# A two-layer encoder trunk: one transfer for four weight blocks, a fixed order of the MLP's products, narrower projection products, and products ahead of the head whose result nobody reads

## The chip, the cores and the metric

The kernel runs on one core of a Trainium2 chip. The metric is the device time of one execution in microseconds (us). The profile is one execution, taken by the hardware profiler. In it PE is TensorE's products, PEld its loading of stationary operands, DVE VectorE, ACT ScalarE, POOL GpSimd and SP SyncE, which issues most transfers.

## The reference

```python
def reference(x, mem, mem_norm, attn_norm, mlp_norm, a_w_in, a_rpb, b_w_in, b_q_norm,
              b_k_norm, w_mem_kv, w_o, w_up, w_down, final_norm):
    m = rms_norm(mem, mem_norm)
    h = x
    for i in range(DEPTH):                       # DEPTH = 2
        n = rms_norm(h, attn_norm[i])
        j = i // N_MIXERS
        if i % N_MIXERS == 0:
            z = n @ a_w_in[j]                    # 2048 x 5120
            q, k, v, qm = jnp.split(z, [MIX_WIDTH, 2 * MIX_WIDTH, 3 * MIX_WIDTH], axis=-1)
            mix = neighbourhood_attention(...)   # 12 heads of 128, learned relative bias
        else:
            z = n @ b_w_in[j]                    # 2048 x 3072
            ...
            mix = gqa_block_attention(q, k, split_heads(v, N_KV_HEADS))
        km, vm = jnp.split(m @ w_mem_kv[i], 2, axis=-1)
        cross = memory_attention(...)            # 4 heads into 256 memory tokens
        h = h + jnp.concatenate([mix, cross], axis=-1) @ w_o[i]
        n = rms_norm(h, mlp_norm[i])
        h = h + jnp.square(jax.nn.relu(n @ w_up[i])) @ w_down[i]   # 2048 x 8192 and back
    return rms_norm(h, final_norm)
```

All is float32, with 256 tokens of width 2048.

## The kernel before

Every matrix product is made of three products of a rounded type: each operand is split into a high part (a rounding copy on ScalarE) and a low part (the difference, on VectorE), and high by high, high by low and low by high are added up in PSUM. The function `split` issues this pair; in the profile all of its copies stand on line 329 and all of its differences on line 330. Weights come in chunks of 128 x 2048 (1 MB), are loaded by SP's queue, split in two halves, and used once.

The work is a list of grains. A grain runs a part of a chunk's products; ahead of it, by a fixed number of grains, its load is issued (8 ahead), its sums (`pre`, 5 ahead) and its split (4 ahead). A scheduler may then move instructions on each engine; `pin` keeps an instruction in the program's order on its engine.

There are three kinds of products. An **S** chunk gives 128 output features for all 256 tokens: the weights are stationary, the activations move, and for each of 16 k-tiles (`s_products`, lines 240 to 251) there is one 512-wide product of the weights' high part with both parts of the activations (line 247) and one 256-wide product of the low part (line 250). The two halves of the PSUM tile are then added by `summed` (lines 368 to 376). There are 36 such chunks: the memory keys of both layers, and queries, keys and memory queries of layer A. An **M** chunk has the activations stationary and the weights moving, 512 wide (lines 234, 237, 238): values, all of layer B's projections, the output projection and the last part of the MLP's way down. In the **MLP** (`up_grains`, `down_grains`) the way up is like an S chunk, but with three 256-wide products a k-tile (lines 735 and 736). The way down uses a scheme with seven products in place of eight (names p1 to p7, lines 849 to 851), on sums of weight blocks.

The hidden width is cut in eight parts. The first part's up chunks stand alone; then come 56 steps a layer, each with one up chunk (48 products, 256 wide) and one down step (21 products, 512 wide). A down step takes four weight blocks of 128 x 512. Three of them are loaded into `b` (768 KB), the fourth into `t` (256 KB). `pre` adds one block to the fourth on VectorE (line 828) and lets a transfer of POOL's queue add another one in place (line 829, called the accumulating transfer here). `prep_first` splits the three blocks (bh, bl), `prep_second` makes two more sums (lines 837, 838) and splits four (th, tl). Both tiles have two buffers in turn; bh, bl, th and tl have one each. The first products (three names, nine products) use bh and bl, the second (four names, twelve products) th and tl.

At the start, `begin` splits the memory tokens and the first three S chunks in quarters. Their loads are issued by SP in the order written; the first quarter of each of the three weight chunks is issued by ScalarE (line 142).

Of the kernel before, what the change touches and what calls it, by code (L numbers as in the profile page):

```python
# [17 lines left out]
P = 128  # L18
# [17 lines left out]
GROUP = 2  # L36
# [8 lines left out]
LAST_AT = 224  # L45
MASKED = -1e30
# [21 lines left out]
class Shifted:  # L68
# [5 lines left out]
    def __getitem__(self, key):  # L74
        _, k, s = key
        at = k * 512 + (s.start or 0)
        if k == KT - 1:

            at = k * 512 + (0 if s.start else SEQ + LAST_AT // 4)
        return self.room[:, at : at + SEQ]  # L80

# [9 lines left out]
def encoder_kernel(ctx: ExitStack, tc: tile.TileContext, t: dict, out: bass.AP):  # L91
# [62 lines left out]
    nc.scalar.activation(warm, mhalf[:, :1], AF.Exp)  # L154

# [10 lines left out]
    def halves_of(w):  # L166
# [9 lines left out]
        def prep(hf):  # L176
# [7 lines left out]
            tiles[hf] = new_half()  # L184
            split(*tiles[hf], tiles["raw"][:, hf * HALF : (hf + 1) * HALF])
# [23 lines left out]
    def new_half():  # L209
        return (at.ring.tile([P, HALF], F32R, tag="hi", bufs=4, name="hi"),  # L210
                at.ring.tile([P, HALF], F32R, tag="lo", bufs=4, name="lo"))
# [28 lines left out]
    def s_products(w, k0, nk, hi, lo):  # L240

        acts, ps = w.acts(), w.ps
        for j0 in range(0, nk, GROUP):
            js = range(j0, min(j0 + GROUP, nk))
            for j in js:
                s = slice(j * P, (j + 1) * P)
                nc.tensor.matmul(ps, hi[:, s], acts[:, k0 + j, :], start=k0 + j == 0, stop=False)  # L247
            for j in js:
                s = slice(j * P, (j + 1) * P)
                nc.tensor.matmul(ps[:, SEQ:], lo[:, s], acts[:, k0 + j, :SEQ], start=False,  # L250
                                     stop=k0 + j == KT - 1)

    def begin():
# [5 lines left out]
        for q in range(4):  # L259
            for k in range(4 * q, 4 * q + 4):  # L260
                split_pair(box["memT"], mem0[:, k * SEQ : (k + 1) * SEQ], G_MEM, k)
                if k % 4 == 0:
                    for c, w in enumerate(plan[:FIRST_CHUNKS]):
                        if q % 2 == 0:
                            tiles[c] = new_half()
# [33 lines left out]
    def add_s(src, acts, done):  # L299
        def start(w):  # L300
            w.ps = at.acc.tile([P, 512], F32, tag="acc", name="ps_s")
# [66 lines left out]
    def summed(ps, name, row=None, factor=1.0):  # L368

        a = at.work.tile([P, SEQ], F32, tag="sum_a", name=f"{name}_a")  # L370
        nc.scalar.activation(a, ps[:, SEQ:], AF.Copy)
        s = at.work.tile([P, SEQ], F32, tag="sum_s", name=f"{name}_s")
        nc.vector.tensor_tensor(s, ps[:, :SEQ], a, op=ALU.add)
        if row is not None:
            nc.vector.scalar_tensor_tensor(s, s, factor, row, op0=ALU.mult, op1=ALU.mult)
# [142 lines left out]
    def add_mem(layer):  # L518
        for hd in range(NMH):
            add_s(t[f"w_km{layer}"][hd], get("memT"), km_done(layer, hd))  # L520
# [206 lines left out]
    def u_products(ps, k0, nk, hi, lo):  # L727

        acts = box["hT"]
        for j in range(nk):  # L730
            k = k0 + j
            s = slice(j * P, (j + 1) * P)
            parts = (slice(0, SEQ), slice(SEQ, 512))
            for n, x in enumerate(parts if k < KT - 1 else parts[::-1]):
                nc.tensor.matmul(ps, hi[:, s], acts[:, k, x], start=k == n == 0, stop=False)  # L735
            nc.tensor.matmul(ps, lo[:, s], acts[:, k, :SEQ], start=False, stop=k == KT - 1)  # L736
# [12 lines left out]
    def up_grains(layer, part, m):  # L749
# [8 lines left out]
        def run(hf):  # L758
            if hf == 0:
                if part == 0:  # L760
                    own["ps"] = at.acc.tile([P, 512], F32, tag="acc", name="ps_u")[:, :SEQ]
                else:
                    if part == 1 and m == 0:
                        closed("ps_att", "ps_acc")
                        at.sums = opened("ps_sums", space=bass.MemoryType.PSUM)
                        box["ps"] = {}
                        box["unused"] = set()
# [513 lines left out]
```

## Time and profile before

| | us |
|---|---|
| median of 3 runs | 2047.32 |
| the runs | 2046.80, 2047.32, 2050.19 |
| the profiled execution's own time | 2048.19 |
| its span, first to last instruction | 2046.4 |

The mean granted TensorE clock of the profiled execution was 0.998. A line of a group gives source line, engine, operation, the tile written and those read, shape and count, then the busy time in us, the mean of one in ns, and the engine's idle time just before them with what ended it. A line of the timeline gives start and length in us, engine, line and what is done, and how many are merged in it. A line of a stretch gives its ends, its length, then busy time and count for each engine, the granted clock, the mean busy share of the DMA engines, and GB/s.

### The profile page before, as it was taken

Reading aid. Unit: us, or ns where it says so; the run is one execution under the profiler, and the core shown is the slowest. Engines: PE = TensorE matmul, PEld = TensorE weight load, DVE = VectorE, ACT = ScalarE, POOL = GpSimd, SP = SyncE. Lnnn points to the kernel's source line nnn. Section 1 sums busy time; section 2 is a strip of 40 time slices with the busy share of each in tenths; the row PEclk is TensorE's granted clock in tenths of the full one; section 3 lists DMA queues with packets and bytes.
Section 4 is the critical chain, followed back from the end, with each engine's and each line's share of the span. In section 5 each row is a group of like instructions: output and inputs, shape, how many; then the busy total and the mean of one; then the engine's idle time right before and its main releaser. Section 6 shows DMA issues by size and latency. Waiting matters only on the chain.

```text
span 2046.4 us, 31582 instructions
## 1 busy us (share of the span) xinstructions
PE 2026.7 (99%) x12516; PEld 1813.8 (89%) x12516; DVE 1667.0 (81%) x2061; ACT 1251.6 (61%) x1652; POOL 119.2 (6%) x144
## 2 busy tenths in 40 slices
PE   8999999999999999999999999999999999999998
PEld 7888888889999999999988888889999999999996
DVE  6767667558989989999897667657998989999996
ACT  6755555556666666666656557556666666666664
POOL 0000000000000000000000001000000000000000
PEclk9999999999999999999999999999999999999999
DMA  7755554727777777787775554536877777777773
GB/s 281 283 190 179 191 177 169 277 80 233 231 231 232 220 232 230 226 242 222 230 222 199 180 185 144 184 125 216 246 227 227 227 231 229 234 232 227 236 221 130
DMA packets 93429, 433.79 MB, mean 212 GB/s; under 512 B 10464, under 2 KB 12128, under 8 KB 60128
## 3 DMA queue, kind: packets, MB, share of 16 engines
q1 hardware_dynamic: 75456, 398.47, 57.3%
q0 software_dynamic: 16816, 31.46, 8.7%
q8 instruction: 98, 1.61, 0.3%
q10 hardware_dynamic: 1008, 1.84, 0.3%
q14 instruction: 51, 0.42, 0.1%
HBM read 398.17 MB, written 4.19 MB: 197 GB/s over the span
## 4 chain that ended last, share of the span: by engine, by line
PE 93%; DVE 3%; DMA 2%; issue 1%; ACT 0%; POOLq 0%; POOL 0%; SPq 0%; DVEq 0%; ACTq 0%
PE ps_u L735 21%; PE ps_u L736 11%; PE ps_m L234 8%; PE ps_m L237 8%; PE ps_m L238 8%; PE p L849 8%; PE p L850 8%; PE p L851 8%; PE ps_s L247 7%; PE ps_s L250 3%; DMA t<-in_w_pair 1%; DVE tl L330 1%; PE pt_a L410 1%; DVE ul L330 1%; PE pt_n L347 1%
## 5 line engine op out<-in xcount | busy, mean ns | idle before, releaser
L735 PE MATMUL ps_u<-hT,uh 128*128 128x256 f32 x4096 | 713.2, 278 | 0.2
L735 PEld LDWEIGHTS ps_u<-hT,uh 128*128 128x128 f32 x4096 | 627.4, 188 | 10.3 <-ACT uh L329 0.6
L736 PE MATMUL ps_u<-hT,ul 128*128 128x256 f32 x2048 | 568.9, 278 | 1.6 <-DVE ul L330 1.5
L329 ACT ACTIVATE uh<-raw_U 128x1024 fp32r<-128x1024 f32 x278 | 294.6, 1061 | 307.1 <-PE ps_u L735 290.0
L330 DVE TENSOR_TENSOR lo<-raw,hi 128x1024 fp32r<-128x1024 f32 (+1 forms) x220 | 261.4, 1194 | 164.5 <-ACT hi L329 162.9
L736 PEld LDWEIGHTS ps_u<-hT,ul 128*128 128x128 f32 x2048 | 386.2, 189 | 4.2 <-DVE ul L330 3.2
L330 DVE TENSOR_TENSOR ul<-raw_U,uh 128x1024 fp32r<-128x1024 f32 x278 | 337.3, 1218 | 40.6 <-ACT uh L329 40.5
L329 ACT ACTIVATE hi<-raw 128x1024 fp32r<-128x1024 f32 (+1 forms) x220 | 227.5, 1039 | 210.2 <-PE ps_m L238 119.1
L329 ACT ACTIVATE th<-t 128x2048 fp32r<-128x2048 f32 x112 | 215.2, 1921 | 118.7 <-PE p L851 107.8
L330 DVE TENSOR_TENSOR tl<-t,th 128x2048 fp32r<-128x2048 f32 x112 | 256.0, 2286 | 23.9 <-ACT th L329 23.5
L330 DVE TENSOR_TENSOR bl<-b,bh 128x1536 fp32r<-128x1536 f32 x112 | 196.0, 1750 | 0.3 <-ACT bh L329 0.3
L850 PE MATMUL p<-tl,a_s 128*128 128x512 f32 x448 | 174.8, 390 | 0.0
L851 PE MATMUL p<-th,a_s 128*128 128x512 f32 x448 | 174.3, 389 | 0.0
L329 ACT ACTIVATE bh<-b 128x1536 fp32r<-128x1536 f32 x112 | 166.2, 1484 | 7.3 <-PE p L851 1.2
L829 POOL DMA_DIRECT2D t<-b x112 | 97.0, 866 | 1158.8 <-DVE t L828 556.0
L849 PE MATMUL p<-th,a_s 128*128 128x512 f32 x448 | 164.1, 391 | 0.0
L247 PE MATMUL ps_s<-nT,hi 128*128 128x512 f32 x448 | 142.5, 397 | 0.0
L851 PE MATMUL p<-bh,a_s 128*128 128x512 f32 x336 | 131.1, 390 | 0.0
L850 PE MATMUL p<-bl,a_s 128*128 128x512 f32 x336 | 131.0, 390 | 0.0
L828 DVE TENSOR_TENSOR t<-t,b 128x512 f32<-128x512 f32 x112 | 77.2, 689 | 57.6 <-DMA t<-in_w_pair 46.5
L849 PE MATMUL p<-bh,a_s 128*128 128x512 f32 x336 | 108.0, 389 | 0.0
L237 PE MATMUL ps_m<-lo,nT 128*128 128x512 f32 x264 | 103.7, 393 | 0.0
(237 smaller groups left out, 3305.1 us busy)
## 6 DMA issues: line engine op xcount, KB each, us to landing
raw_U<-in_w_up SPq DMA_DIRECT2D x128, 1024.0 KB, 6.6
b<-in_w_pair SPq DMA_DIRECT2D x112, 768.0 KB, 4.5
raw<-in_w_o SPq DMA_DIRECT2D x32, 1024.0 KB, 5.0
t<-in_w_pair SPq DMA_DIRECT2D x112, 256.0 KB, 3.4
t<-b POOLq DMA_DIRECT2D x112, 256.0 KB, 6.9
raw<-in_w_b SPq DMA_DIRECT2D x21, 1024.0 KB, 4.9
raw<-in_w_av SPq DMA_DIRECT2D x12, 1024.0 KB, 4.9
raw<-in_w_aq SPq DMA_DIRECT2D x12, 1024.0 KB, 4.9
```

What stands on the lines that cost most here:

```text
L234: first = nc.tensor.matmul(w.ps[i], ah, hi[:, s], start=st, stop=False)
L237: nc.tensor.matmul(w.ps[i], ah, lo[:, s], start=False, stop=False)
L238: nc.tensor.matmul(w.ps[i], al, hi[:, s], start=False, stop=sp)
L247: nc.tensor.matmul(ps, hi[:, s], acts[:, k0 + j, :], start=k0 + j == 0, stop=False)
L329: first = nc.scalar.activation(dst_hi, src, AF.Copy)
L330: return first, nc.vector.tensor_tensor(dst_lo, src, dst_hi.bitcast(F32), op=ALU.subtract)
L735: nc.tensor.matmul(ps, hi[:, s], acts[:, k, x], start=k == n == 0, stop=False)
L736: nc.tensor.matmul(ps, lo[:, s], acts[:, k, :SEQ], start=False, stop=k == KT - 1)
L829: nc.gpsimd.dma_start(s[:, 0, :], block(1), accum_op=ALU.add)
L849: nc.tensor.matmul(ps, a[:, 0, ai, :], hi[:, s], start=begins, stop=False)
L850: nc.tensor.matmul(ps, a[:, 0, ai, :], lo[:, s], start=False, stop=False)
L851: nc.tensor.matmul(ps, a[:, 1, ai, :], hi[:, s], start=False, stop=ends)
```

## The change

- The four blocks of a down step come in one transfer of 1 MB into `b`. All sums are made in `pre`, into a tile `t` of three; the accumulating transfer adds into the fourth block of `b`. The first split takes all four blocks (2048 wide) and the first products are four names (p3, p1, p2, p5); the second split takes three sums (1536 wide) for three names.
- A step's grains are ordered down first, up first half, up second half, down second, and the first product of each group is pinned in the program's order.
- S chunks use the same three 256-wide products as the way up, into one 256-wide sum, so `summed` needs no addition. Their split tiles lie 64 bytes into a somewhat longer buffer. The first half of an S chunk that follows an M chunk starts with its low part, which is laid out apart (`Entered`). Two of the first four chunks share a PSUM bank.
- At the start, SP issues all first loads; twelve 128 x 128 products of a tile of ones are issued ahead of all others, into a PSUM tile that is not read.
- The last part's second chunks are loaded into the buffers of `b` in place of those of `T`.

```diff
             for c in range(FIRST_CHUNKS):
-                (nc.sync if j else nc.scalar).dma_start(raws[c][:, s], t["w_km0"][c][:, s])
+                nc.sync.dma_start(raws[c][:, s], t["w_km0"][c][:, s])
...
+    idle = at.att.tile([P, P], F32, tag="att", name="idle")
+    for _ in range(12):
+        nc.tensor.matmul(idle, ones, ones, start=True, stop=True)
...
+            if w.kind == "S" and hf == 0 and plan[plan.index(w) - 1].kind == "M":
+                tiles[hf] = entered_half(src)
+            else:
+                tiles[hf] = new_half(w.kind)
+                split(*tiles[hf], src)
...
+    def new_half(kind):
+        s = slice(STILL_AT // 4, STILL_AT // 4 + HALF) if kind == "S" else slice(0, HALF)
+        return tuple(at.ring.tile([P, HALF + 64], F32R, tag=n, bufs=4, name=n)[:, s] for n in ("hi", "lo"))
+
+    def entered_half(src):
+        hi = at.ring.tile([P, HALF + 64], F32R, tag="hi", bufs=4, name="hi")[:, STILL_AT // 4 :][:, :HALF]
+        lo = Entered(at.ring.tile([P, HALF + 64], F32R, tag="lo", bufs=4, name="lo"))
+        nc.scalar.activation(hi, src, AF.Copy)
+        for dst, s in ((lo.first, slice(0, P)), (lo.rest, slice(P, HALF))):
+            nc.vector.tensor_tensor(dst, src[:, s], hi[:, s].bitcast(F32), op=ALU.subtract)
+        return hi, lo
...
+    def products(ps, acts, k0, nk, hi, lo, keep_order=False):
+        for j in range(nk):
+            k = k0 + j
+            s = slice(j * P, (j + 1) * P)
+            parts = [(hi, slice(0, SEQ)), (hi, slice(SEQ, 512)), (lo, slice(0, SEQ))]
+            if k == KT - 1:
+                parts[:2] = parts[1::-1]
+            elif j == 0 and isinstance(lo, Entered):
+                parts = parts[2:] + parts[:2]
+            for n, (x, part) in enumerate(parts):
+                ins = nc.tensor.matmul(ps, x[:, s], acts[:, k, part], start=k == n == 0,
+                                       stop=k == KT - 1 and n == 2)
+                if keep_order and n == 0:
+                    pin(ins)
...
-    FIRST = ("p3", 6, 0), ("p1", 0, 1), ("p2", 2, 2)
-    SECOND = ("p5", 3, 0), ("p7", 4, 1), ("p6", 5, 2), ("p4", 1, 3)
+    FIRST = ("p3", 6, 0), ("p1", 0, 1), ("p2", 2, 2), ("p5", 3, 3)
+    SECOND = ("p7", 4, 0), ("p6", 5, 1), ("p4", 1, 2)
...
-            own["b"] = at.side.tile([P, 3 * 512], F32, tag="b", bufs=2, name="b")
-            nc.sync.dma_start(own["b"], src[:, : 3 * 512])
-            own["t"] = at.side.tile([P, 4, 512], F32, tag="T", bufs=2, name="t")
-            nc.sync.dma_start(own["t"][:, 0, :], src[:, 3 * 512 :])
+            own["b"] = at.side.tile([P, 4, 512], F32, tag="b", bufs=2, name="b")
+            nc.sync.dma_start(own["b"].rearrange("p a b -> p (a b)"),
+                              t[f"w_pair{layer}"][(part * 2 + q) * STEPS + j])
...
         def pre():
-            s = own["t"]
-            nc.vector.tensor_tensor(s[:, 1, :], s[:, 0, :], block(0), op=ALU.add)
-            nc.gpsimd.dma_start(s[:, 0, :], block(1), accum_op=ALU.add)
+            b, s = own["b"], at.side.tile([P, 3, 512], F32, tag="T", bufs=2, name="t")
+            nc.vector.tensor_tensor(s[:, 0, :], b[:, 3, :], b[:, 0, :], op=ALU.add)
+            nc.gpsimd.dma_start(b[:, 3, :], b[:, 1, :], accum_op=ALU.add)
+            nc.vector.tensor_tensor(s[:, 1, :], s[:, 0, :], b[:, 1, :], op=ALU.add)
+            nc.vector.tensor_tensor(s[:, 2, :], s[:, 1, :], b[:, 2, :], op=ALU.add)
+            own["t"] = s
...
-            plan.extend((up[0], down[0], up[1], down[1]))
+            plan.extend((down[0], up[0], up[1], down[1]))
```

The switch of the PSUM pools moves from the first up grain of the second part to the first down grain. In the programs as they are built, TensorE's order of an ordinary step is the same circle before and after: before, twelve second products of one step, nine first products of the next, 48 up products; after, twelve first products, 48 up products, nine second products.

More of the change, by code (lines that the diff above doesn't have):

```diff
@@ L762, in run @@
                 else:
[L763 to L767, printed above, removed]
                     own["ps"] = at.sums.tile([P, 512], F32, tag="up", name="ps_u")[:, :SEQ]
[L769 removed]
+            products(own["ps"], box["hT"], hf * (KT // 2), KT // 2, *own.pop(hf), keep_order=part > 0)
         def after():
```

78 lines of the change are left out of this document (30 added, 48 removed).

## The prediction

> **What bounds the kernel now.** I read the page first, then the times of the stretches, then the groups of the MLP stretch, and last the timeline of the places that the change touches. The page says who is busy and what the chain to the end is made of.
>
> ```profile
> span 2046.4 us, 31582 instructions
> PE 2026.7 (99%) x12516; PEld 1813.8 (89%) x12516; DVE 1667.0 (81%) x2061; ACT 1251.6 (61%) x1652; POOL 119.2 (6%) x144
> PE 93%; DVE 3%; DMA 2%; issue 1%; ACT 0%; POOLq 0%; POOL 0%; SPq 0%; DVEq 0%; ACTq 0%
> ```
>
> TensorE sets the time nearly everywhere. A change can gain only by starting TensorE earlier, by spacing its products closer, or by removing the few waits that it has. It can lose where the next engine in line comes late, and that is VectorE in the MLP. Below is the MLP stretch: the busy times of an ordinary 100 us of it, the VectorE groups of 490 to 1035 us, and two starts of the same place in two steps that follow each other.
>
> ```profile
> core 0: us, PE busy (x) PEld busy (x) DVE busy (x) ACT busy (x) POOL busy (x), PEclk, DMA share, GB/s
> 600.00:700.00 100.00, 100.00 (x671) 91.74 (x670) 91.74 (x103) 66.71 (x69) 8.70 (x10) 1.00 0.79 233
> ```
> ```profile
> L330 DVE TENSOR_TENSOR tl<-t,th 128x2048 fp32r<-128x2048 f32 x53 | 121.2, 2286 | 11.6 <-ACT th L329 11.3
> L330 DVE TENSOR_TENSOR bl<-b,bh 128x1536 fp32r<-128x1536 f32 x53 | 92.7, 1750 | 0.0
> L828 DVE TENSOR_TENSOR t<-t,b 128x512 f32<-128x512 f32 x52 | 35.9, 690 | 30.4 <-DMA t<-in_w_pair 24.3 <-issue 3.0 <-DVE ul L330 2.9
> L838 DVE TENSOR_TENSOR t<-t,b 128x512 f32<-128x512 f32 x53 | 36.3, 684 | 0.2
> ```
> ```profile
> 522.47 0.40 PE L735 MATMUL ps_u<-hT,uh 128*128 128x256 f32 x2
> ...
> 528.18 0.39 PE L850 MATMUL p<-tl,a_s 128*128 128x512 f32 x1
> ...
> 530.45 0.39 PE L851 MATMUL p<-th,a_s 128*128 128x512 f32 x1
> ...
> 532.72 0.40 PE L735 MATMUL ps_u<-hT,uh 128*128 128x256 f32 x2
> ```
>
> One step takes TensorE 532.72 - 522.47 = 10.25 us, and its 512-wide products follow each other at 0.227 us (ten of them from 528.18 to 530.45). VectorE is busy 91.7% of it, 9.4 us, and of its 0.85 us of slack it spends 24.3 / 53 = 0.46 us waiting for the separate transfer of the fourth block. TensorE idles nowhere in that row. So the MLP is bound by TensorE with VectorE 0.85 us behind it, in each of 112 steps (two layers, 56 each).
>
> **Part 1, the head.** The change sends all first quarters through SP in one order (memory tokens first, then the three weight chunks), and puts twelve unread products ahead of the head.
>
> ```profile
> 0.72 0.20 POOL L150 MEMSET ones<- 128x128 f32 x1 [0.29 <-POOLq L1271]
> ...
> 4.84 0.63 ACT L329 ACTIVATE hi<-raw 128x512 fp32r<-128x512 f32 x1 [1.21 <-DMA raw<-in_w_km]
> ...
> 6.91 0.91 ACT L355 ACTIVATE memT<-h,gains 128x256 fp32r<-128x256 f32 x2 [1.44 <-DMA h<-in_memT]
> ...
> 7.99 1.65 PE L247 MATMUL ps_s<-memT,hi 128*128 128x512 f32 x3 [7.99 <-DVE memT L356]
> ```
> ```profile
> 7.99:12.40 4.41, 4.41 (x12) 1.00 1.05 383
> 12.40:26.00 13.60, 13.60 (x79) 1.00 1.04 416
> ```
>
> The first weights land at 4.84 us, the first memory tokens only just before 6.91 us, because they share the way with two more weight quarters. In one queue the tokens are first; at 383 GB/s a 256 KB transfer takes 0.7 us, so tokens land at about 4.9 and the first weights at 5.6 to 6.2 us. With the 0.63 us of the split TensorE starts at about 6.6 instead of 7.99 us: -1.4 us. The bounds are 0 (SP also has to issue the three transfers that ScalarE's queue issued before) and -2.1 us (the landing at 4.84 us shifts all).
>
> The two stretches show the cold clock: 12 products in 4.41 us, then 79 in 13.60 us. The 12 are eight 512-wide and four 256-wide ones. At the warm spacing, 0.227 us and half of it, they would take 2.3 us, so 2.1 us are lost. The unread products can take that loss away only if they keep TensorE busy for about as long as those 4.41 us. The nearest row is the plain f32 product of the norms, 256 wide and warm:
>
> ```profile
> 53.65 0.59 PE L365 MATMUL pt_r<-diag,ones 128*128 128x256 f32 x2
> 53.89 0.58 PE L238 MATMUL ps_m<-hi,memT 128*128 128x512 f32 x1
> 54.31 0.39 PE L234 MATMUL ps_m<-hi,memT 128*128 128x512 f32 x1
> ```
>
> From 53.65 to 54.31 us stand this product and one of 0.23 us, so it costs 0.43 us; half as wide and at half the clock it again costs 0.43 us. Twelve take 5.1 us, from the memset's end at 0.92 to about 6.1 us, and delay nothing, since TensorE waited until 7.99 us anyway. 5.1 us is more than 4.41 us, so I take the whole -2.1 us; the other end is 0. [...]
>
> Head together: -3.5 us, bounds 0 and -4.2.
>
> **Part 2, projections as three 256-wide products.** 36 chunks of 16 k-tiles had a 512-wide product and a 256-wide one each; now three 256-wide ones. The columns are the same. Before, the timeline gives six pairs of k-tiles between these starts; the MLP's up products, which already have the new form, give nine and thirteen k-tiles in the two stretches below them (busy times there are L735's alone).
>
> ```profile
> 235.68 0.63 PE L247 MATMUL ps_s<-nT,hi 128*128 128x512 f32 x2
> ...
> 239.86 0.40 PE L247 MATMUL ps_s<-nT,hi 128*128 128x512 f32 x1
> ```
> ```profile
> 458.66:461.84 3.18, 3.18 (x19) 1.00 0.95 307
> 523.18:527.60 4.42, 4.42 (x27) 1.00 0.84 258
> ```
>
> That is 4.18 / 12 = 0.348 us a k-tile before, and in the new form either 3.18 / 9 = 0.353 or 4.42 / 13 = 0.340 us. [...] Over 576 k-tiles the ends are +2.9 and -4.6 us. I take 0.344 us, nearer the fast pace because the offsets are new, but not at it, since attention products break the runs: -2.5 us. [...]
>
> The ScalarE copy and the VectorE sum that joined the two halves go away; both engines had room there, so nothing is counted.
>
> **Part 3, the MLP's order on TensorE.** Before, the scheduler pulled two up products ahead of the down products wherever a column half ended, and the rest of that run then went at the slow pace. One of these places, with the two pulled products first and then thirteen k-tiles between two starts:
>
> ```profile
> 787.97 0.40 PE L735 MATMUL ps_u<-hT,uh 128*128 128x256 f32 x2
> 788.21 0.39 PE L850 MATMUL p<-bl,a_s 128*128 128x512 f32 x1
> ...
> 790.06 0.40 PE L735 MATMUL ps_u<-hT,uh 128*128 128x256 f32 x2
> ...
> 794.65 0.40 PE L735 MATMUL ps_u<-hT,uh 128*128 128x256 f32 x2
> ```
>
> 4.59 / 13 = 0.353 against 0.340 us: 0.2 us a run. By the code a half ends once in each of the seven parts of a layer that have a down step, 14 times in all: about 2.4 us with the piece before. In the changed program all 112 up runs are whole (48 products in a row) between 21 down products, so this goes: -2.2 us, bounds 0 and -2.8. The order of a step stays a circle of 48 and 21, so the number of switches is the same.
>
> **Part 4, four blocks in one transfer.** The work on VectorE and ScalarE is the same in sum: the 2048-wide split is now that of the first products, the 1536-wide one that of the second, and three sums of 0.69 us stay. What changes is who waits for what.
>
> ```profile
> raw_U<-in_w_up SPq DMA_DIRECT2D x128, 1024.0 KB, 6.6
> b<-in_w_pair SPq DMA_DIRECT2D x112, 768.0 KB, 4.5
> raw<-in_w_o SPq DMA_DIRECT2D x32, 1024.0 KB, 5.0
> t<-in_w_pair SPq DMA_DIRECT2D x112, 256.0 KB, 3.4
> t<-b POOLq DMA_DIRECT2D x112, 256.0 KB, 6.9
> ```
> ```profile
> L329 ACT ACTIVATE th<-t 128x2048 fp32r<-128x2048 f32 x112 | 215.2, 1921 | 118.7 <-PE p L851 107.8
> ```
>
> ```profile
> 600.37 0.69 DVE L828 TENSOR_TENSOR t<-t,b 128x512 f32<-128x512 f32 x1
> ...
> 601.58 0.87 POOL L829 DMA_DIRECT2D t<-b  x1 [9.64 <-ACT c L790]
> ```
> ```profile
> PEld ps_u L736 <- DVE ul L330: 0.5, 1, 0.5
> ```
> ```profile
> L789 ACT ACTIVATE c<-ps_u 128x256 f32<-128x256 f32 x128 | 46.6, 364 | 0.0
> ```
>
> In the changed order VectorE does, each step: first sum of step n+1, split low of step n's blocks, the other sums, two up splits, split low of step n's sums. Step n+2's transfer may start when the blocks of step n are split. This makes a circle: load L, first sum 0.69, in every second step one more sum (0.35 on average), split 2.29: L + 3.3 us. It must stay below 10.25 us, so L may be up to 6.9 us. L is not shown. A bound below is 5.0 (1 MB with little beside it), a scaled one 4.5 x 4/3 = 6.0 us, and 6.6 us, the upper end, is what raw_U takes beside the accumulating transfer. I take 5.6 us, near the same data's own row: 1.3 us to spare.
>
> The accumulating transfer (POOL's queue) now stands before the first products. It is issued 0.5 us after the end of the first sum, lands 6.9 us later, then ScalarE needs 1.92 us: 9.4 us, and one step is 10.25 us. Behind the waiting split on ScalarE are the up splits. They are not late at once: the split may start when the first products of the step before are done, and between that and its own products lie 48 + 9 products, 5.44 + 2.05 = 7.5 us, for 1.92 + 2.29 = 4.2 us of work. So TensorE has 3.3 us of cover here. I count 0.
>
> The wait of 0.46 us a step for the fourth block goes with its transfer; VectorE has slack, so that is worth only TensorE's waits in the MLP, and the chain of waits shows one of 0.5 us in the first layer's: -0.5 us, bounds 0 and -1.0. At the first down step the PSUM tiles of the first up part are taken over at once, which can cost up to one evacuation (0.36 us) a layer and its signal: I take +0.25 us a layer, +0.5 us, bounds 0 and +1.0.
>
> **Sum.** -3.5 - 2.5 - 2.2 - 0.5 + 0.5 = -8.2 us. The profiled execution took 2048.19 us, 1.8 us more than its span and 0.9 us above the median of the runs, 2047.32. A head start counts in full, since TensorE is the bound from 26 us on. From the median: **2039.1 us**. All good ends together give -4.2 - 4.6 - 2.8 - 1.0 = -12.6 us, 2034.7 us.
>
> **Rivals.** (a) *The load circle becomes the bound: slower.* The 1 MB load now runs beside the accumulating transfer, and both are slowed by sharing. For it: raw_U's 6.6 us beside it against 5.0 alone. Against it: the accumulating transfer is issued about 2 us before the load, so they share only a part. It decides from L = 6.9 us. At 7.5 us each step would be 0.55 us longer, 112 x 0.55 = 62 us; 2047 + 62 - 8 = 2101 us. Chance 0.17, with milder forms of it.
>
> (b) *The spacing and the clock do not follow.* The projections fall into the slow pace (+2.9 instead of -2.5) and the unread products do not raise the clock (2.1 us less): -8.2 + 5.4 + 2.1 = -0.7 us, 2046.6 us. For it: the long up runs of the first part show the slow pace in the very form that is used. [...] Chance of this or one half of it that lands within 0.2%: 0.14.
>
> **Numbers.** A measurement of this kernel can tell about 0.2%, 4.1 us, from no change. Forecast (below 2043.2 us): 0.69; within: 0.14; slower: 0.17. The range goes from 2033 us to 2052 us: it holds the forecast, case (b) and the mildest of (a), and leaves most of (a) out.
>
> **What would show it.** Right: the first projection product at about 6.6 us at full spacing; 0.340 to 0.348 us a k-tile in the projections; all up runs at 0.340 us; steps of 10.25 us; VectorE's first sum waiting little for the load. Wrong: a first sum that waits over 0.9 us in most steps, TensorE idle before the first down products, or a step longer than 10.3 us.

## The result, and the profile after

| | kernel before | changed kernel |
|---|---|---|
| median of the runs, us | 2048.76 (2046.80 to 2051.72, 4 runs) | 2064.55 (2061.64 to 2065.99, 4 runs) |
| the profiled execution, us | 2048.19 | 2065.99 |
| its span, us | 2046.4 | 2064.2 |

The changed kernel is slower: 1.0074 times the time before, 95% interval 1.0056 to 1.0092, about 16 us. The forecast was 2039.1 us, in a range that ended at 2052.

The page of the changed kernel: span, busy times, the chain of work that ended last, and the DMA issues (KB each, median us from issue to landing).

```profile
span 2064.2 us, 32575 instructions
PE 2034.1 (99%) x13116; PEld 1844.1 (89%) x13116; DVE 1663.7 (81%) x2030; ACT 1243.8 (60%) x1616; POOL 119.3 (6%) x144
PE 73%; DVE 1%; DMA 1%; issue 1%; ACT 1%; POOLq 0%; POOL 0%; ACTq 0%; DVEq 0%
raw_U<-in_w_up SPq DMA_DIRECT2D x128, 1024.0 KB, 5.1
b<-in_w_pair SPq DMA_DIRECT2D x112, 1024.0 KB, 5.1
b<-b POOLq DMA_DIRECT2D x112, 256.0 KB, 3.4
```

VectorE's and ScalarE's sums are about as before (3 and 8 us less), and TensorE's grew by 7.4 us, though its products, the unread ones aside, have the same number of columns in sum. The chain is followed back only to 471.97 us here, where it stops at an accumulating transfer b<-b. Its shares therefore add up to 77% of the span, and TensorE's 73% cannot be set against the 93% of the kernel before. The load that the prediction feared, b<-in_w_pair, lands after 5.1 us. The accumulating transfer lands after 3.4 us, not 6.9.

An ordinary 100 us of the MLP, and VectorE's groups of 495 to 1040 us (busy us, mean ns, then idle time before them and what ended it):

```profile
core 0: us, PE busy (x) PEld busy (x) DVE busy (x) ACT busy (x) POOL busy (x), PEclk, DMA share, GB/s
600.00:700.00 100.00, 100.00 (x673) 91.81 (x673) 92.78 (x99) 65.62 (x68) 8.71 (x10) 1.00 0.73 226
L371 DVE TENSOR_TENSOR bl<-b,bh 128x2048 fp32r<-128x2048 f32 x53 | 121.3, 2289 | 6.5 <-ACT bh L370 6.5
L845 DVE TENSOR_TENSOR t<-b 128x512 f32<-128x512 f32 x52 | 35.8, 688 | 3.7 <-DMA b<-in_w_pair 3.2
```

The steady MLP is what was forecast. TensorE does not idle in this stretch, and the first sum waits 3.2 us for its load in 52 steps, where it waited 24.3 us before. So the loss must lie at single places, and a table of where TensorE stands finds them. Each number is the start of a product in the timeline, in us; the last column is the best kernel of the experiments below.

| product | before | changed | difference | best |
|---|---|---|---|---|
| first of the projections | 7.99 | 6.16 | -1.8 | 6.48 |
| first of the norms (pt_m) | 46.14 | 43.90 | -2.2 | 43.49 |
| layer 0: first up product | 442.01 | 437.86 | -4.2 | 437.45 |
| its first down product | 489.89 | 491.72 | +1.8 | 484.87 |
| first of the 5th down step | 530.68 | 533.85 | +3.2 | 526.59 |
| first of the 55th down step | 1044.98 | 1046.52 | +1.5 | 1039.25 |
| first plain product | 1066.17 | 1069.10 | +2.9 | 1059.76 |
| layer 1: first up product | 1370.71 | 1373.76 | +3.1 | 1364.36 |
| its first down product | 1418.51 | 1428.08 | +9.6 | 1411.72 |
| first of the 5th down step | 1459.31 | 1469.23 | +9.9 | 1454.00 |
| first of the 55th down step | 1973.08 | 1983.61 | +10.5 | 1966.67 |
| first plain product | 1993.93 | 2010.00 | +16.1 | 1987.17 |
| last product | 2037.22 | 2055.02 | +17.8 | 2030.47 |

Up to the MLP 4.2 us are gained, and the steady steps gain in both layers: 10.25 us each (in layer 1 without a wait of 1.7 us just ahead of the 55th) instead of 10.28 to 10.29. Each start of the MLP loses 7 us (from -4.2 to +3.2, from +3.1 to +9.9), the last two steps of layer 1 about 6 (1.7 of it stands ahead of the 55th step's first product), each end 1.4, and the plain stage of layer 1 another 1.7.

**The start of the MLP.** First the chain of waits of layer 0's start, then ScalarE's timeline there.

```profile
471.97 5.06 DMA b<-b
477.05 1.93 ACT bh L370
481.21 1.22 DVE ul L371
486.30 1.14 DVE ul L371
487.49 4.29 PE ps_u L286 x21
```
```profile
477.05 1.92 ACT L370 ACTIVATE bh<-b 128x2048 fp32r<-128x2048 f32 x1 [1.25 <-DMA b<-b]
478.87 1.04 ACT L370 ACTIVATE uh<-raw_U 128x1024 fp32r<-128x1024 f32 x1
479.82 1.47 ACT L370 ACTIVATE th<-t 128x1536 fp32r<-128x1536 f32 x1
```

Before there was no such chain. On ScalarE bh, the split of the first down step, waits 1.25 us for the accumulating transfer, and behind it in the order stands uh, the split of an up chunk that TensorE needs at once. Both kernels hold the splits of the first two down steps behind the fourth newest up split, and no further. VectorE does bl, tl and a split of activations ahead of the same chunk's low parts (ul, which end at 482.4 and 487.4 us). TensorE waits 2.2 and 2.1 us for them. The five largest groups of waits of TensorE and its weight load (PEld) from 440 to 2055 us, with the sum in us, how many, and the longest; one stop can stand in both a PE and a PEld row:

```profile
PEld ps_u L286 <- DVE ul L371: 9.6, 7, 2.2
PE ps_u L286 <- DVE ul L371: 8.1, 7, 2.0
PEld ps_m L265 <- ACT h_p L370: 4.6, 2, 2.3
PE ps_m L265 <- DVE h L905: 3.8, 2, 1.9
PEld p L871 <- ACT c L811: 2.5, 2, 1.5
```

**The clock.** The 21 products that the chain shows from 487.49 us take 4.29 us, nearly twice the 2.4 us that they take at 0.340 us for three, as measured at full clock. Two of the four stretches in which the granted clock (PEclk) was one half:

```profile
487.72:491.13 3.41, 3.41 (x18) 3.41 (x18) 3.38 (x5) 0.00 (x0) 0.87 (x1) 0.50 0.82 246
2010.06:2013.48 3.42, 3.42 (x8) 2.67 (x9) 3.39 (x6) 0.00 (x0) 0.00 (x0) 0.50 0.83 297
```

Each of the four lasts 3.41 us and comes right behind a wait that puts 2.20 to 2.33 us between the starts of two products, and costs up to 1.7 us on top of it.

**The end of the MLP.** The last down product and the first plain one of layer 0:

```profile
1066.80 0.39 PE L873 MATMUL p<-th,a_s 128*128 128x512 f32 x1
1069.10 0.47 PE L265 MATMUL ps_m<-uh,a_p 128*128 128x512 f32 x1 [1.91 <-DVE h L905]
```

The instruction that writes h at line 905 takes the sum p4 out of PSUM. Through the moved switch of the pools, p4 is the first tile of the MLP's pool and lies in the first bank, and this is where the first plain sum goes. Before, the first tile was the up tile, free long before.

**The last steps of layer 1.** The same place in both layers, layer 0 first: the accumulating transfer's issue, the next load's, and the split that waits for the former.

```profile
1037.08 0.87 POOL L846 DMA_DIRECT2D b<-b  x1 [14.14 <-DVE t L845]
1038.31 0.33 SPq L773 DMA_DIRECT2D raw_U<-in_w_up  x1
1041.17 1.92 ACT L370 ACTIVATE bh<-b 128x2048 fp32r<-128x2048 f32 x1 [3.21 <-DVE z L930]
1973.12 0.86 POOL L846 DMA_DIRECT2D b<-b  x1 [14.82 <-DVE z L929]
1973.68 0.33 SPq L773 DMA_DIRECT2D raw_U<-in_w_up  x1
1981.65 1.91 ACT L370 ACTIVATE bh<-b 128x2048 fp32r<-128x2048 f32 x1 [8.32 <-DMA b<-b]
```

VectorE folds a finished column half here (lines 928 and 929), and the first sum comes late, so the transfer is issued 5 us later in the step than in the steps ahead of it. In layer 0 it still lands in time. In layer 1 the next load follows after 0.56 us instead of 1.23, and the split can start only 8.5 us after the transfer's issue.

### The profile page after: what moved, and what is told of

It reads as the page before. It is cut to its first block, busy times and chain, and to the rows that moved or that the text cites. A ratio compares the mean times of both kernels' runs of the same rounds, so it can differ in the third digit from the quotient of the medians.

```text
span 2064.2 us, 32575 instructions
## 1 busy us (share of the span) xinstructions
PE 2034.1 (99%) x13116; PEld 1844.1 (89%) x13116; DVE 1663.7 (81%) x2030; ACT 1243.8 (60%) x1616; POOL 119.3 (6%) x144
## 4 chain that ended last, share of the span: by engine, by line
PE 73%; DVE 1%; DMA 1%; issue 1%; ACT 1%; POOLq 0%; POOL 0%; ACTq 0%; DVEq 0%
PE ps_u L286 31%; PE p L871 9%; PE p L872 9%; PE p L873 8%; PE ps_m L265 5%; PE ps_m L268 5%; PE ps_m L269 5%; DMA b<-b 1%; DVE ul L371 1%; PE pt_n L388 0%; PE pt_a L447 0%; DMA raw_U<-in_w_up 0%; ACT bh L370 0%; ACT uh L370 0%; PE pt_h L1087 0%
## 5 line engine op out<-in xcount | busy, mean ns | idle before, releaser
L370 ACT ACTIVATE bh<-b 128x2048 fp32r<-128x2048 f32 x112 | 215.2, 1922 | 122.3 <-PE p L873 87.7
L371 DVE TENSOR_TENSOR bl<-b,bh 128x2048 fp32r<-128x2048 f32 x112 | 256.3, 2289 | 22.2 <-ACT bh L370 22.1
L371 DVE TENSOR_TENSOR tl<-t,th 128x1536 fp32r<-128x1536 f32 x112 | 196.7, 1756 | 42.1 <-ACT th L370 41.1
L370 ACT ACTIVATE th<-t 128x1536 fp32r<-128x1536 f32 x112 | 166.7, 1488 | 38.7 <-PE p L873 38.7
L871 PE MATMUL p<-bh,a_s 128*128 128x512 f32 x448 | 175.2, 391 | 3.5 <-ACT c L811 1.9
L873 PE MATMUL p<-bh,a_s 128*128 128x512 f32 x448 | 175.3, 391 | 0.0
L846 POOL DMA_DIRECT2D b<-b x112 | 97.0, 866 | 1157.0 <-DVE t L845 902.7
L286 PE MATMUL ps_s<-nT,hi 128*128 128x256 f32 x896 | 158.1, 279 | 0.0
L286 PEld LDWEIGHTS ps_s<-nT,hi 128*128 128x128 f32 x896 | 136.3, 188 | 0.2
L871 PE MATMUL p<-th,a_s 128*128 128x512 f32 x336 | 131.4, 391 | 0.0
L873 PE MATMUL p<-th,a_s 128*128 128x512 f32 x336 | 130.7, 389 | 0.0
L286 PE MATMUL ps_s<-nT,lo 128*128 128x256 f32 x448 | 124.9, 279 | 0.0
```

Source lines behind the costliest of these rows:

```text
L286: ins = nc.tensor.matmul(ps, x[:, s], acts[:, k, part], start=k == n == 0, stop=k == KT - 1 and n == 2)
L370: first = nc.scalar.activation(dst_hi, src, AF.Copy)
L371: return first, nc.vector.tensor_tensor(dst_lo, src, dst_hi.bitcast(F32), op=ALU.subtract)
L846: nc.gpsimd.dma_start(b[:, 3, :], b[:, 1, :], accum_op=ALU.add)
L871: pin(nc.tensor.matmul(ps, a[:, 0, ai, :], hi[:, s], start=begins, stop=False))
L873: nc.tensor.matmul(ps, a[:, 1, ai, :], hi[:, s], start=False, stop=ends)
```

## The experiments

The theory after this result: head, projections and steady MLP do what was forecast; the loss is at the MLP's borders, by the order on ScalarE and VectorE at its start, by a PSUM bank at its end, and by the folds. The rivals were that head and projections give their gain back later, that the plain chunk's load through other buffers causes the wait at the end, and that the accumulating transfer is late whatever stands where. The times of the kernel before, in the same sessions, were 2047.3, 2048.0, 2047.9 and 2047.3 us (medians).

**The MLP put back (mlp_as_before).** FIRST, SECOND, the two transfers, the order of the grains and the buffers of the plain chunk as before.

```diff
-            plan.extend((down[0], up[0], up[1], down[1]))
+            plan.extend((up[0], down[0], up[1], down[1]))
...
-                     t[f"w_pair{layer}"][(part * 2 + q) * STEPS + j])
+            nc.sync.dma_start(own["b"], src[:, : 3 * 512])
+            nc.sync.dma_start(own["t"][:, 0, :], src[:, 3 * 512 :])
```

> The changed kernel with its MLP (order of the grains, loads, sums, first and second products, buffers of the last part) put back as it was before; the head and the projections stay changed. Theory A (the loss lies in the MLP alone; head and projections gain what the landmark 'first up product' shows, 442.01 to 437.86 us): about 4.2 us below the kernel before, near 2044 us, and TensorE's first down product of layer 0 near 485.7 us. [...]

2051.34 us (2046.26 to 2057.10), 1.0019 (1.0009 to 1.0029). Theory A falls: the first up product came at 437.38 us, 4.6 earlier than before, but at the end the kernel stood 3.2 us behind. By the medians the new MLP costs 13 us (11 by the two ratios), not the 20 us that A's 2044 us would have left for it. The old one loses some 8 us here that it doesn't lose in the kernel before, in steps spread over both layers. ScalarE's split of the second products, 500 to 1040 us, in the kernel before and in this one:

```profile
L329 ACT ACTIVATE th<-t 128x2048 fp32r<-128x2048 f32 x53 | 101.8, 1921 | 56.9 <-PE p L851 50.9 <-DVE ul L330 3.2 <-DVE bl L330 1.7
L370 ACT ACTIVATE th<-t 128x2048 fp32r<-128x2048 f32 x52 | 99.9, 1921 | 62.4 <-PE p L889 44.0 <-DMA t<-b 14.0 <-DVE ul L371 4.3
```

The new wait is for the accumulating transfer, 14.0 us. So two kernels asked which part brings that about.

**The head alone (head_only)**, on the kernel before.

```diff
-                (nc.sync if j else nc.scalar).dma_start(raws[c][:, s], t["w_km0"][c][:, s])
+                nc.sync.dma_start(raws[c][:, s], t["w_km0"][c][:, s])
...
+    idle = at.att.tile([P, P], F32, tag="att", name="idle")
+    for _ in range(12):
+        nc.tensor.matmul(idle, ones, ones, start=True, stop=True)
```

> The kernel before with the head's change alone (all first loads through SP, twelve unread products). In the kernel with the head and the projections changed and the old MLP, TensorE reached the MLP 4.6 us earlier, but lost 7.8 us in it. Theory A (the old MLP has VectorE and its loads close behind TensorE; a head start of TensorE uses up that slack, and the accumulating transfers fall late, in a part of the runs): the first up product about 2 us earlier than before, and of that little or nothing left at the end: within 2 us of the kernel before, with runs that differ by several us. Rival B (a head start counts in full; what was lost there has to do with the projections): 2 us below the kernel before, 2045.3 us, runs close together.

2046.03 us (2044.59 to 2048.32), 0.9988 (0.9979 to 0.9997). This is nearer to rival B: in the profiled execution, one of the fastest, the 2.7 us that the first up product comes earlier are kept, and more, to the end (span 2043.0 us). Over the runs it is 2 us, at the edge of what theory A allowed, and the runs are not close together.

**The projections alone (projections_only)**, on the kernel before: `products`, `Entered`, the offsets and `summed` as changed, head and MLP as before.

```diff
-                nc.tensor.matmul(ps, hi[:, s], acts[:, k0 + j, :], start=k0 + j == 0, stop=False)
...
+            parts = [(hi, slice(0, SEQ)), (hi, slice(SEQ, 512)), (lo, slice(0, SEQ))]
```

> The kernel before with the projections' change alone (three 256-wide products, 64 bytes of offset, one sum in place of two). Theory A (the projections gain 2 us ahead of the MLP, but their other timing or places bring the old MLP into its slower course, as in the kernel with head and projections): first up product about 2 us earlier than before, 439.5 to 440 us, and the end 2 to 4 us later, runs spread over several us. Rival B (it takes head and projections together to do that): 2045.5 to 2046 us, as the head alone did.

2046.85 us (2046.27 to 2049.50), 0.9997 (0.9988 to 1.0005). Theory A falls: the end is not later. It is nearer to rival B, at a gain of 1 us that can't be told from none. So each part alone leaves the old MLP in its course, and both together do not. Why stays open; no run here tells more than that the accumulating transfer comes late in it.

**Another order of the PSUM tiles (banks)**, in the changed kernel: the up tile first, p7, p6 and p4 next.

```diff
+                box["up"] = at.sums.tile([P, 512], F32, tag="up", name="ps_u")
...
-            for x in ("p4", "p3", "p1", "p2", "p5", "p7", "p6"):
+            for x in ("p7", "p6", "p4", "p3", "p1", "p2", "p5"):
```

> The changed kernel with another order in which the MLP's PSUM tiles are made: the up tile first, then p7, p6, p4, p3, p1, p2, p5. Theory A (at the end of the MLP the first plain product waits 2.07 us because its bank is the one of p4, which VectorE takes last; at the start p3 or p1 waits for the bank of the last first-part up product): the 2.07 us waits at 1066.8 and 2007.7 us go, and the half clock behind the second one too; 2.3 + 2.3 + 1.7 us, and about 1 us at the two starts: near 2057.5 us. Rival B (the wait comes from the plain chunk's split, whose load now goes through the buffers of b): the waits stay, 2064 us.

2057.14 us (2056.49 to 2060.09), as theory A had it. The end of layer 0, last down and first plain product:

```profile
1066.26 0.39 PE L875 MATMUL p<-th,a_s 128*128 128x512 f32 x1
1066.48 0.39 PE L265 MATMUL ps_m<-uh,a_p 128*128 128x512 f32 x1
```

The wait is gone with the load and its buffers unchanged. The bank was the cause.

**The first splits later (behind).** Splits of the first two down steps behind the newest up split.

```diff
-            return (lambda: past(fn, box["splits"][-4])) if part == 0 and n < 2 else fn
+            return (lambda: past(fn, box["splits"][-last])) if part == 0 and n < 2 else fn
...
...
-        return [Grain(lambda: run("first", FIRST), lambda: after(FIRST), load, behind(pre), behind(prep_first), SOON),
-                Grain(lambda: run("second", SECOND), after_second, None, None, behind(prep_second), SOON)]
+        return [Grain(lambda: run("first", FIRST), lambda: after(FIRST), load, behind(pre), behind(prep_first, 1), SOON),
+                Grain(lambda: run("second", SECOND), after_second, None, None, behind(prep_second, 1), SOON)]
```

> The changed kernel with the splits of the first two down steps of each layer placed behind the newest up split instead of the fourth newest. Theory A (at the MLP's start ScalarE and VectorE do bh, bl, th and tl of the first step ahead of the last first-part up splits, the first of them waiting for the accumulating transfer; TensorE waits 2.18 and 2.09 us for those up splits in layer 0, 2.18 and some smaller ones in layer 1, and the clock halves for 3.4 us in each): these waits and drops go, 5 to 6 us a layer: near 2053.5 us. Rival B (the accumulating transfer is simply late, and the wait moves to the first down products): at most 3 us better, 2061.5 us or more, with TensorE idle before the first p product.

2059.24 us (2056.14 to 2061.44): about half of what A promised. The waits of 2 us for ul are gone, and layer 0's first down product came at 485.84 us, not 491.72. But then TensorE waited at its first down products, in layer 0 and in layer 1:

```profile
PEld p L871 <- ACT c L811: 2.4, 1, 2.4
PEld p L871 <- ACT c L811: 2.9, 1, 2.9
```

c at line 811 empties the last first-part up sum, in the bank that a down sum takes over; it now stands behind other splits on ScalarE.

**Both (banks_behind).**

> The changed kernel with both edits that were run alone, the order of the PSUM tiles (banks) and the later place of the first splits (behind). With behind alone the waits for the up splits went, but TensorE then waited 2.09 us in layer 0 and 2.84 us in layer 1 at its first down products; with banks alone the plain stage began at once. Theory A (what was left with behind is the takeover of a PSUM bank whose evacuation stands behind th on ScalarE): all of these go, 2.1 + 2.8 us at the starts, 2.1 + 2.1 us and two half clocks of 1.7 us at the ends, 12.5 us below the 2059.2 us of behind: near 2047 us. Rival B (the wait at the first down products is for bl or for the accumulating transfer): only the ends gain, 2051.5 us or more.

2054.09 us (2048.87 to 2057.47). The waits for c are gone, as theory A had it, but the time is only 5 us below that of behind alone and not 12, which is in the range of rival B. Two places were left. In layer 1's second down step TensorE now waited for bh and bl, with a half clock behind it. And at the last but one step of layer 1 the wait is larger than in the changed kernel; its waits, 1964 to 1980 us:

```profile
ACT bh L370 <- DMA b<-b: 9.1, 1, 9.1
PEld p L873 <- ACT bh L370: 2.7, 1, 2.7
PEld p L874 <- DVE bl L371: 2.1, 1, 2.1
```

**The folds put off (folds)**, in the changed kernel.

```diff
-            if ends and (part, n) in FOLDS:
-                folded(q)
+            if ends and (part, n) == STEPS_OF[-1]:
+                folded(0)
+                later(6, folded, 1)
```

> The changed kernel with the folds of the first column half put off from its last step (four steps ahead of the MLP's end) to the MLP's end, and those of the second half six grains further. Theory A (in layer 1 the folds on VectorE push the first sum of the last but one step back, the accumulating transfer behind it starts 5 us late, and the split bh with it: 1.72 and 2.10 us of waits and a half clock from 1981.7 to 1989.7 us): 4 to 5.5 us better, near 2059.5 us. Rival B (the transfer itself is slow there, 8.5 us beside two loads, and not its start late): the waits stay to the larger part, 2063 us or more.

2066.51 us (2064.88 to 2067.58). The edit missed its aim: the scheduler put the folds of the first half at the same place on VectorE as before, between the same splits. It says nothing on either theory.

**The folds held (banks_behind_held)**, on banks_behind, with an order that the scheduler must keep.

```diff
-                folded(q)
+                for x in range(2):
+                    later(1 + 6 * x, lambda x=x: past(lambda: folded(x), box["splits"][-1]))
```

> The one before, and the folds of both column halves held behind the up and plain splits at the end of the MLP (the edit that only put them later in the program had left VectorE's order as it was). Theory A (VectorE's folds push the first sum of the last but one step back, so the accumulating transfer is issued late, and within 0.6 us of the next 1 MB load, in which case it takes 7 to 8 us and not 3.4): with the folds out of the way the wait before bh at 1973 to 1981 us goes: 4 to 5 us below the one before. Rival B (the folds only move into the plain stage, where the plain splits then come late): TensorE waits there instead; no gain, or a loss.

2049.04 us (2046.54 to 2051.38), 1.0004 (0.9995 to 1.0013), 5 us below banks_behind, as A had it. In the last steps of layer 1 TensorE waits for no split. At the start of layer 0 this remained:

```profile
DVE t L846 <- DMA b<-in_w_pair: 2.9, 1, 2.9
PEld p L874 <- DVE bl L371: 2.1, 1, 2.1
```

VectorE's next instruction is the third step's first sum; it waits 2.9 us for a 1 MB load that lands after 7.5 us, while two others are on their way, and bl of the second step stands behind it. At both ends TensorE still waited 1.9 us, for p4 once more: the second plain sum takes the fourth bank, where p4 lies since banks (in banks itself it cost at most 0.9 us at each end).

**All borders (best).** Held folds, the order of the tiles mended, and the sums of the third step behind the second step's block split.

```diff
+        def after_blocks():
+            past(pre, box["blocks"])
...
-            for x in ("p7", "p6", "p4", "p3", "p1", "p2", "p5"):
+            for x in ("p4", "p6", "p3", "p1", "p2", "p5", "p7"):
```

> The changed kernel with all edits so far (order of the PSUM tiles, later splits of the first two down steps, held folds) and two more: the PSUM tiles in the order up, p4, p6, p3, p1, p2, p5, p7, since the second plain sum takes the fourth bank and not the second; and the sums of the third down step behind the block split of the second. Theory A (in the kernel with held folds TensorE still waited 1.9 us for p4's bank at both ends, and 1.1 + 2.1 us in layer 0, with a half clock of 1.7 us, and 1.3 us in layer 1 at the second down step, because VectorE's next instruction, the first sum of the third step, waited 2.9 us for a 1 MB load that shares the way with two others): 3.8 + 4.9 + 1.3 us less than 2049.0: near 2039.5 us, ratio to the kernel before 0.996. Rival B (the transfers stay crowded there and something else in line waits for them): 2044 us or more.

2041.64 us (2040.93 to 2044.13), 0.9969 (0.9959 to 0.9979): faster than the kernel before, and some 22 us faster than the changed one. Its page, and the two largest groups of waits of TensorE and its weight load, 440 to 2040 us:

```profile
span 2039.7 us, 32566 instructions
PE 2025.2 (99%) x13116; PEld 1838.6 (90%) x13116; DVE 1661.6 (81%) x2030; ACT 1242.8 (61%) x1616; POOL 119.3 (6%) x144
PE 96%; DVE 1%; ACT 1%; issue 1%; DMA 1%; SPq 0%; POOLq 0%; POOL 0%; ACTq 0%
```
```profile
PEld p L877 <- DVE bl L371: 2.1, 2, 1.3
PEld ps_u L286 <- DVE ul L371: 1.9, 2, 1.0
```

The clock stays at full from 7.2 us on. Of the 2 us above the expectation 1.6 are in the first of these rows: between the products it is 0.5 us at the third down step of layer 0 and 1.1 us at the third of layer 1. Waits like those of the second row, in the first part's up chunks, stood in the kernel before too.

**Without the unread products (no_idle** on banks_behind, **best_no_idle** on best).

```diff
-    idle = at.att.tile([P, P], F32, tag="att", name="idle")
-    for _ in range(12):
-        nc.tensor.matmul(idle, ones, ones, start=True, stop=True)
```

> The kernel with banks and behind, without the twelve products that nobody reads. Theory A (they raise the clock before the first projection product): the first projection product starts at the same time, but the clock stays at half until about 13 us; the products of the norms (46.2 us before the change, 43.9 after) come 2 us later, and the whole takes 2 us more. Rival B (the data sets the pace of the head after the start, so the clock does not matter): the norms' products at the same time as with them, and the same total.

> The best kernel without the twelve products that nobody reads, to price them where no other wait hides it. Theory A (they raise the clock 6 us earlier; 8 or 9 us of products at half clock, less the waits for data that fall into them, are what they save): first projection product as before, the first up product 1.8 to 2.1 us later, and so the whole: 2043.5 us. Rival B (the first data sets the pace of the head, so the clock costs nothing): the same total as the best kernel, 2041.6 us.

2052.04 us (2049.41 to 2055.96) and 2042.30 us (2041.75 to 2043.44). The clock rose at 12.6 and 10.4 us. The first came out 2 us below banks_behind and not above it, with intervals that overlap (1.0008 to 1.0026 against 1.0014 to 1.0035), so the other waits drown the effect. In the second the norms' products come 1.7 us later (45.2 instead of 43.5 us) and the first up product too, near to theory A; at the last product 0.9 us are left, and the medians differ by 0.7 us, which the intervals (0.9963 to 0.9983 against 0.9959 to 0.9979) do not tell apart. So the unread products were worth 1.7 us at the head in these two executions, and for the whole no gain is shown.

**The accumulating transfer beside a load (beside)**, on best.

```diff
+                with tc.issue_after(box["blocks"][1].ins):
+                    nc.gpsimd.dma_start(b[:, 3, :], b[:, 1, :], accum_op=ALU.add)
```

> The best kernel with the accumulating transfer of half of the down steps held back until the block split before it is done; that split also frees the buffer of the next 1 MB load, so both are issued within 0.5 us. Nothing else moves on any engine. Theory A (an accumulating transfer that is issued within 0.9 us of a 1 MB load lands with that load, after 6.5 to 8.5 us, and one with 1.2 us or more ahead of the next load lands after 3.3 to 3.6 us): the held ones take 6.5 to 8.5 us, bh starts 1 to 3 us later in these steps, and TensorE waits in some of them: slower than the best kernel by 5 us or more. Rival B (the time goes with how much the two overlap, by shared bandwidth): 4.5 to 5.5 us, and no wait of TensorE, the same total.

2041.88 us (2041.04 to 2043.11), the same as best, but it decides nothing between the theories: the split that the transfer was put behind is done before the sum that it waits for anyway, so it was issued when it always was. Best and beside at the same place:

```profile
1715.69 0.86 POOL L847 DMA_DIRECT2D b<-b  x1 [6.09 <-DVE t L846]
1715.41 0.86 POOL L851 DMA_DIRECT2D b<-b  x1 [6.09 <-DVE t L846]
```

## Why the prediction was wrong

**Part 1, head: -3.5 us, measured -2.2** at the norms' first product of the two profiles. The start gained more than the 1.4 us counted: 7.99 to 6.16. The clock rose at 6.4 us, as the 12 products were to bring about, but the 2.1 us counted for it were mostly not to be had. At full clock TensorE catches up with the data:

```profile
6.16 0.62 PE L286 MATMUL ps_s<-memT,hi 128*128 128x256 f32 x2
7.32 0.51 PE L286 MATMUL ps_s<-memT,hi 128*128 128x256 f32 x2 [0.54 <-ACT hi L370]
8.81 0.50 PE L286 MATMUL ps_s<-memT,hi 128*128 128x256 f32 x2 [0.53 <-ACT hi L370]
```

The three largest gaps up to 9.9 us add up to 1.7 us. Part of the start belongs to the projections: projections_only starts at 6.95 us with the old loads, where the first product waits for the tokens' high part alone, while in the kernel before it waited for the low part. Nor is the gain sure. In the profiles of banks and folds the clock had risen at 4.9 us, fell back for 3.41 us at 8.3 after TensorE had idled from about 5.7 to 7.3 us, and the norms' first product came at 45.73 and 46.09 us, near the 46.14 of the kernel before; in the other eight profiles with the unread products it came at 43.4 to 44.5 us. That "a head start counts in full" held for the head alone, as far as head_only shows it, but not for head and projections with the old MLP.

**Part 2, projections: -2.5 us for 36 chunks.** From the norms' first product to the first up product it is 395.87 us before and 393.96 after, with 32 of the chunks between: -1.9 us over 512 k-tiles, 3.7 ns each, or 0.344 us a k-tile, the value that was taken. Its reason, the new offsets, is shown by no run. In the changed kernel, behind the head, ten of the unbroken runs of 48 or more products, all at the new offset, go at 0.340 or 0.341 us a k-tile and five at 0.353, so 0.344 is a mix of the two paces, and that it was met so closely is in part luck.

**Part 3, whole up runs: -2.2 us.** The 50 steps from the 5th to the 55th take 1.6 us less in layer 0 and 1.1 us less in layer 1 (leaving out the 1.7 us wait that stands ahead of the 55th there), 2.7 us in all. Right.

**Part 4, the loads: the step that failed.** Its circle was right and had more room than counted: the load lands after 5.1 us (5.6 taken, 6.9 the limit), and rival (a), 2101 us, had no part in the result. The accumulating transfer, taken at 6.9 us, landed after 3.4. What failed is "So TensorE has 3.3 us of cover here. I count 0." That was worked out for an ordinary step and taken for all 112. At the first step of a layer there is no step before it to lend the cover, a new up split is needed every 2.8 us, and the splits of the first step, with their wait for the accumulating transfer, were put ahead of them. The two starts cost 7.3 and 6.9 us. At the last but one step of layer 1 the folds made the transfer late, another 6 us with the clock. The prediction named the rows that would show it ("TensorE idle before the first down products") as signs of an error, but gave them no price.

The other term of that part, the takeover of PSUM tiles, was counted at 0.25 us a layer at the MLP's start alone. It was 0.8 and 1.5 us there, and the moved switch also changed which bank the first plain sum finds at the end: 2.1 us in each layer, and in layer 1 the clock with it.

Rival (b) had no part in this result either: the spacing followed, and the clock rose at 6.4 us and fell for the first time at 487.7 us.

Put together, the gains of head, projections and up runs come to 2.2 + 1.9 + 2.7 = 6.8 us of the 8.2 forecast, and best, where the borders are mended, is 6.3 us below the kernel before. The error that turned a gain into a loss was in the borders, not in the steady parts.

## What to carry to other kernels

A change to a software pipeline must be costed three times: in its steady step, where it fills and where it drains. List for each engine, in its order, what stands ahead of the next thing that TensorE needs at the first and at the last step, and, where pools are opened in another order, which bank the next stage will find and who empties it last. An edit that only moves an instruction in the program may change nothing on the engine; look at the engine's order before measuring it.

## What the runs showed of the hardware

**Six waits of the changed kernel put 2.2 to 2.3 us between two products; behind four of them the clock was at half.** The table has every place from 440 to 2055 us of its profile where the starts of two products that follow each other lie more than 1.5 us apart, in us, with the granted clock (PEclk) behind it.

| starts of the two products | apart | clock behind |
|---|---|---|
| 480.19, 482.48 | 2.29 | 1.00 |
| 485.29, 487.49 | 2.20 | 0.50 from 487.72 to 491.13 |
| 1066.80, 1069.10 | 2.30 | 1.00 |
| 1416.68, 1418.98 | 2.29 | 0.50 from 1419.56 to 1422.97 |
| 1426.50, 1428.08 | 1.58 | 1.00 |
| 1981.66, 1983.61 | 1.95 | 1.00 |
| 1983.61, 1985.94 | 2.33 | 0.50 from 1986.17 to 1989.58 |
| 2007.70, 2010.00 | 2.30 | 0.50 from 2010.06 to 2013.48 |

In the stretch from 1986.17 us the 512-wide products follow each other at 0.43 us, at full clock at 0.227, so a stretch of 3.41 us costs up to 1.7 us on top of the wait ahead of it. The wait at the end of the MLP is 2.30 us from start to start in both layers, and cost no clock in layer 0 and 1.7 us in layer 1. What decides between the two is shown by no run.

**When an accumulating transfer landed went with the loads that were issued near it.** In the kernel before, 63 of the 112 were followed by the next load within 0.6 to 0.9 us and took 7.1 us (median), and 35 were followed after 1.2 to 1.6 us and took 3.6 us. In the changed kernel 84 had 1.6 to 2.5 us ahead of the next load and took 3.3 us; the one with 0.56 us took 8.4. Another 23 had still more room, but all but one of them had a load issued 1.1 to 3.6 us ahead of them, and they took 5.0 us. So the 6.9 us that the prediction took from the page did not hold in the new neighbourhood. No edit of these runs moved a transfer across that gap by itself, so this is what the traces show together, not a tested cause.
